# One Trainium2 core, attention block with mixture of experts: w_out kept whole and split early, token tiles of the output product finished one by one, diff-head work moved off VectorE, expert loads chained

## The chip, the cores and the metric

The program runs on one core of one Trainium2 chip. The metric is device time in microseconds (us) for one execution; the median of three runs is given. A profile of one execution comes with it: busy time of TensorE (PE, its weight loads PEld), VectorE (DVE), ScalarE (ACT), GpSimd (POOL), the queue of SyncE (SP) that issues most DMAs, and what the 16 DMA engines moved.

## The reference

One encoder layer, batch 1, 512 tokens, width 1024, all float32. Cut to what matters:

```python
h = rms_norm(x, attn_norm_w)
z = h @ w_in                       # 1024 x 5664: c_q, c_kv, k_rope, dq, dk, dv, g_mla, g_diff
o_mla  = latent_attention(...)     # 16 heads, width 64
# differential attention: 8 heads, two softmax maps of width 64 each, value width 128
a = softmax(q1 k1^T/8 - slope*|t-s|) - lam * softmax(q2 k2^T/8 - slope*|t-s|)
o_diff = rms_norm(a @ v, diff_subln_w) * (1 - lam_init)      # per head
merged = sigmoid(g_mla + b) * o_mla + sigmoid(g_diff + b) * o_diff
x = x + merged @ w_out             # 1024 x 1024
h2 = rms_norm(x, ffn_norm_w)
affinity = softmax(h2 @ router_w)  # 16 experts
gate, idx = top_k(affinity^T, 64)  # every expert picks its 64 tokens
for e in range(16):                # width 1024 -> 2048 -> 1024
    ye = (silu(h2[idx[e]] @ w_gate[e]) * (h2[idx[e]] @ w_up[e])) @ w_down[e] * gate[e]
    x[idx[e]] += ye
```

The expert weights are 16 x 3 x 8 MB, 402.7 MB in all, and each byte is read once.

## The kernel before

Products ahead of the routing are made in three matmuls each (`proj3`): both operands are split into a rounded part `hi` and a rest `lo`, and hi*hi, hi*lo and lo*hi are summed. A weight is split after it is loaded: ScalarE copies the hi part (L129, for diff weights L516), VectorE or GpSimd subtracts it for lo (L130, L517).

The program goes through these stages: projections and the 16 latent-attention heads with the gates (to about 315 us); differential attention, 8 heads (to 576 us); the product with `w_out` (`wo`, 518 to 609 us); routing and top-k (to 630 us); the experts (to the end).

**Differential heads.** A generator `proj` makes the projections `dqkv` of a head, one token tile of 128 tokens (24 matmuls) at a step, ahead of the attention of that head; it is 7 token tiles ahead when the first head starts. A head transposes its keys and queries (`kT` L550, `qT` L554), splits them (`KH`, `KL`, `QS`, the copy L560 on GpSimd), and for each of 4 token tiles t makes scores `S`, the biased maximum (L579), two exponentials (L581), the difference (L587, `pr`), the transposes `ATp`, copied out as `AT` (ScalarE for odd t, VectorE for even), and `pvd`. GpSimd makes the bias (L571) and the normed `qk` (L536). A head ends with `o` scaled by its norm (L610), transposed (`oT` L613), gated (L614) and added into `mrg` (L615), the merged output, transposed, one 128x512 tile for each head.

**w_out.** The weight is loaded in quarters of each half n of its columns, and split; `mt` is the hi and lo of `mrg` in pieces (L716 ScalarE, L717 VectorE). For n = 0 all token tiles are taken with the first seven k, then with the last, which is head 7's; for n = 1 the tiles t follow one another, 24 matmuls each, and each goes on to its residual sum (L745), transposes `xmT`, logits `lg` and affinities.

**Experts.** The weights come as 384 chunks of 1 MB, each in a slot of a ring. `ORDER` gives the 22 slots by letter: m, e, a, h, b, c, x are memory regions that become free at different times. All chunk loads (L702) go through SP's queue, in the order of use; a load waits until the last reader of its slot is done, and what stands behind it in the queue waits too. The four h slots hold `mt`, one token tile each. An expert takes 24 chunks: 16 for gate and up (`gu`), 8 for down (`y`).

Of the kernel before, what the change touches and what calls it, by code (L numbers as in the profile page):

```python
# [31 lines left out]
ORDER = "eeeemmaxaaaahhhhbbbbbc"  # L32
NRE, NRA, NRB = (ORDER.count(c) for c in "eab")
# [13 lines left out]
def build(tc, A, out):  # L47
# [41 lines left out]
    with ExitStack() as es:  # L89
# [9 lines left out]
        wpool = prj.enter_context(tc.tile_pool(name="w", bufs=1, reuse_waits="tile"))  # L99
# [406 lines left out]
        def diff_proj(h):  # L506
# [27 lines left out]
            eng = V if h == 0 else G  # L534
# [10 lines left out]
        def diff_head(h, qkv, qk2, gB):  # L545
# [22 lines left out]
            for t in range(NT):  # L568
# [36 lines left out]
        def finish(h, o, oss, gB):  # L605
# [20 lines left out]
        xm = xpool.tile([128, NT, D], F32, name="xm")  # L626
        for t in range(NT):
            SY.dma_start(xm[:, t], x_in[t * 128:(t + 1) * 128])
# [19 lines left out]
        pb.__exit__(None, None, None)  # L648
        pb3.close()

# [4 lines left out]
        wpool = att.enter_context(tc.tile_pool(name="wo", bufs=1, reuse_waits="tile"))  # L655

        def wo_view(n, i):
            return w_out[:, 2 * i:2 * i + 2, n * 512:(n + 1) * 512]

        def wo_split(n):  # L660
            return [w_split(wo_view(n, i), (128, 2, 512), eng=G if n == 0 and i == 3 else None,
                            raw=raw1[:, i - 2] if n == 1 and i > 1 else None) for i in range(4)]

        sc = wpool.tile([NE, 1024], F32, name="sc")
        wo0 = wo_split(0)
        mt_ = [ringH.tile([128, 2, KT, 128], F32R, name="mt", tag="wh", bufs=NT) for _ in range(NT)]
# [8 lines left out]
        rings = {"m": (lambda: mpool, "m8", 2), "e": (lambda: ringE, "we", NRE), "a": (lambda: ringA, "wa", NRA),  # L675
                 "b": (lambda: ringB, "wb", NRB), "h": (lambda: ringH, "wh", NT), "c": (lambda: ringC, "wc", 1),
                 "x": (lambda: ringX, "wx", 1)}
# [4 lines left out]
        def slot_tile(pool, tag, n, shape=(128, FF)):  # L682
            return pool().tile(list(shape), F32, name="w" + tag, tag=tag, bufs=n)

        def chunks():

            i = 0
            for e in range(NE):
# [3 lines left out]
                for src in srcs:  # L692
                    pool, tag, n = rings[order[i]]
                    i += 1
                    w = slot_tile(pool, tag, n)
                    if len(src.shape) == 3:
                        w = w.rearrange("p (j d) -> p j d", j=2)
                    if e == NE - 1 and src is srcs[-1]:
                        for j in range(2):
                            SY.dma_start(w[:, j], src[:, j])  # L700
                    else:
                        SY.dma_start(w, src)  # L702
                    yield w

        stream = chunks()
        early = [next(stream) for _ in range(5)]
        raw1 = slot_tile(*rings["a"], shape=(128, 2, 2, 512))
        for i in range(2):
            SY.dma_start(raw1[:, i], wo_view(1, 2 + i))
        early += [next(stream) for _ in range(2)]  # L710
# [75 lines left out]
        for n in range(2):  # L786
            wo = wo0 if n == 0 else wo_split(1)
            if n == 0:
                wps = [ps_tile(g_, "wo") for g_ in ("pj", "pj", "s", "s")]
                for ks in (range(7), range(7, 8)):  # L790
                    for t in range(NT):
                        wo_part(wps[t], t, wo, ks)
# [227 lines left out]
```

## Time and profile before

| | |
|---|---|
| median of 3 runs | 1559.41 us (1558.34 to 1559.48) |
| profiled execution, time | 1559.79 us |
| its span | 1558.1 us |
| PE / DVE / ACT / POOL busy | 1429.8 / 566.7 / 376.9 / 157.1 us |
| HBM read / written | 441.57 / 5.77 MB |

The span is what the trace holds between first and last instruction; the execution's own time is 1.7 us longer. In the rows below, busy time is a sum over instructions, a row's "idle before" is what its engine waited just ahead of it, and the name behind the arrow is what ended that wait. Matmul durations overlap, so the spacing of their starts is the rate.

### The profile page before, as it was taken

Reading aid. Unit: us, or ns where it says so; the run is one execution under the profiler, and the core shown is the slowest. Engines: PE = TensorE matmul, PEld = TensorE weight load, DVE = VectorE, ACT = ScalarE, POOL = GpSimd, SP = SyncE. Lnnn points to the kernel's source line nnn. Section 1 sums busy time; section 2 is a strip of 40 time slices with the busy share of each in tenths; the row PEclk is TensorE's granted clock in tenths of the full one; section 3 lists DMA queues with packets and bytes.
Section 4 is the critical chain, followed back from the end, with each engine's and each line's share of the span. In section 5 each row is a group of like instructions: output and inputs, shape, how many; then the busy total and the mean of one; then the engine's idle time right before and its main releaser. Section 6 shows DMA issues by size and latency. Waiting matters only on the chain. (4 is left out here: it accounts for less than half of the span.)

```text
span 1558.1 us, 18428 instructions
## 1 busy us (share of the span) xinstructions
PE 1429.8 (92%) x7119; PEld 778.1 (50%) x7119; DVE 566.7 (36%) x1412; ACT 376.9 (24%) x830; POOL 157.1 (10%) x213
## 2 busy tenths in 40 slices
PE   7999999999999897999999979889979979979876
PEld 6777767689888675434343333233224224215211
DVE  8965656448888887102102002002002002002100
ACT  4555545546565642000000000000000000000000
POOL 3003303023434410000000000000000000000000
PEclk9999999999999998999999999999999999999999
DMA  4412213132222268899999999999999999999997
GB/s 157 136 44 62 58 51 104 34 92 69 58 58 55 76 254 317 326 420 425 420 420 425 419 420 425 423 422 422 420 423 423 419 424 423 422 424 419 420 418 287
DMA packets 125690, 448.55 MB, mean 288 GB/s; under 512 B 9733, under 2 KB 51777, under 8 KB 92578
## 3 DMA queue, kind: packets, MB, share of 16 engines
q1 hardware_dynamic: 124160, 444.30, 71.7%
q0 software_dynamic: 1440, 3.07, 0.7%
q8 instruction: 56, 0.92, 0.2%
q14 instruction: 32, 0.26, 0.1%
q10 hardware_dynamic: 2, 0.00, 0.0%
HBM read 441.57 MB, written 5.77 MB: 287 GB/s over the span
## 5 line engine op out<-in xcount | busy, mean ns | idle before, releaser
L962 DVE TENSOR_TENSOR hh<-hh,gu 128x512 f32<-128x512 f32 x32 | 22.0, 687 | 433.3 <-PE gu L950 433.3
L950 PE MATMUL gu<-wwa,xeT 128*64 128x512 f32 x560 | 131.5, 605 | 13.6 <-DMA wwa<-in_expert_w_up_dram 7.0
L950 PE MATMUL gu<-wwb,xeT 128*64 128x512 f32 x520 | 121.6, 599 | 15.7 <-DMA wwb<-in_expert_w_up_dram 8.2
L950 PE MATMUL gu<-wwe,xeT 128*64 128x512 f32 x496 | 117.9, 603 | 15.5 <-DMA wwe<-in_expert_w_up_dram 8.9
L950 PE MATMUL gu<-wwh,xeT 128*64 128x512 f32 x432 | 101.3, 599 | 11.3 <-DMA wwh<-in_expert_w_gate_dram 6.5
L959 ACT ACTIVATE hh<-gu 128x512 f32<-128x512 f32 x32 | 19.0, 597 | 344.6 <-PE gu L950 344.6
L950 PEld LDWEIGHTS gu<-wwa,xeT 128*64 128x64 f32 x560 | 37.8, 137 | 103.0 <-issue 66.0
L201 PE MATMUL dqkv<-hl,hTh 128*128 128x384 f32 x256 | 88.5, 346 | 0.2 <-DVE hl L517 0.2
L200 PE MATMUL dqkv<-hl,hTh 128*128 128x384 f32 x256 | 87.3, 342 | 0.0
L889 POOL DMA_DIRECT2D out_dram<-acc x4 | 2.2, 558 | 830.0 <-DVE acc L885 830.0
L202 PE MATMUL dqkv<-hl,hTl 128*128 128x384 f32 x256 | 85.5, 338 | 0.0
L950 PEld LDWEIGHTS gu<-wwb,xeT 128*64 128x64 f32 x520 | 34.6, 136 | 100.5 <-issue 59.6
L983 PE MATMUL y<-wwb,hh 128*64 128x512 f32 x320 | 74.1, 599 | 7.2 <-DMA wwb<-in_expert_w_down_dram 7.2
L950 PEld LDWEIGHTS gu<-wwe,xeT 128*64 128x64 f32 x496 | 32.6, 137 | 94.6 <-issue 53.3
L970 ACT ACTIVATE hh<-hTp 128x512 f32<-128x512 f32 x16 | 9.6, 598 | 277.4 <-PE hTp L967 277.4
L950 PEld LDWEIGHTS gu<-wwh,xeT 128*64 128x64 f32 x432 | 28.7, 136 | 80.8 <-issue 51.1
L983 PE MATMUL y<-wwa,hh 128*64 128x512 f32 x280 | 63.7, 597 | 4.0 <-DMA wwa<-in_expert_w_down_dram 4.0
L911 PE MATMUL xeTp<-ohr,xm 128*128 128x128 f32 x512 | 62.6, 282 | 1.3 <-DVE ohr L898 1.3
L911 PEld LDWEIGHTS xeTp<-ohr,xm 128*128 128x128 f32 x512 | 59.8, 196 | 7.6 <-issue 6.3
L882 PE MATMUL comb<-yo 128*128 128x512 f32 x112 | 57.4, 625 | 4.1 <-ACT yo L995 4.1
L996 DVE COPY yo<-y 64x512 f32<-64x512 f32 x14 | 9.7, 694 | 140.3 <-ACT yo L995 140.3
L983 PE MATMUL y<-wwh,hh 128*64 128x512 f32 x240 | 55.1, 598 | 3.5 <-DMA wwh<-in_expert_w_down_dram 3.5
(356 smaller groups left out, 2548.4 us busy)
## 6 DMA issues: line engine op xcount, KB each, us to landing
wwb<-in_expert_w_down_dram SPq DMA_DIRECT2D x39, 1024.0 KB, 18.0
wwa<-in_expert_w_gate_dram SPq DMA_DIRECT2D x36, 1024.0 KB, 19.8
wwb<-in_expert_w_up_dram SPq DMA_DIRECT2D x35, 1024.0 KB, 19.5
wwa<-in_expert_w_down_dram SPq DMA_DIRECT2D x35, 1024.0 KB, 19.9
wwa<-in_expert_w_up_dram SPq DMA_DIRECT2D x34, 1024.0 KB, 19.8
wwe<-in_expert_w_gate_dram SPq DMA_DIRECT2D x32, 1024.0 KB, 19.6
wwb<-in_expert_w_gate_dram SPq DMA_DIRECT2D x30, 1024.0 KB, 19.6
wwe<-in_expert_w_up_dram SPq DMA_DIRECT2D x30, 1024.0 KB, 19.6
```

The costliest lines, as they stand in the source:

```text
L200: PE.matmul(p, sh, mh, start=first and k == 0, stop=False)
L201: PE.matmul(p, sh, ml, start=False, stop=False)
L202: PE.matmul(p, sl, mh, start=False, stop=last and k == n - 1)
L882: PE.matmul(p, ohT[:, t * 128:(t + 1) * 128], ysp[:, n], start=True, stop=True)
L889: G.dma_start(out2[t * 128:(t + 1) * 128], acc[t // 2][:, t % 2])
L911: PE.matmul(p[:, k], xm[:, t, kk * 128:(kk + 1) * 128], ohr[:, t].rearrange("p a s -> p (a s)"), start=t == 0, stop=t == NT - 1)
L950: PE.matmul(pp[j][hf * 64:(hf + 1) * 64], cur[:, k, par_ * 64:(par_ + 1) * 64], wt[:, hf * 1024 + j * 512:hf * 1024 + (j + 1) * 512], star ...
L959: S.activation(hid[:, j * 512:(j + 1) * 512], pp[j], AF.Silu)
L962: V.tensor_tensor(hs, hs, gu[1][j], OP.mult)
L970: S.activation(dst, p, AF.Copy)
L983: PE.matmul(y[a * 64:(a + 1) * 64], hT[:, f, hf * 64:(hf + 1) * 64], wt[:, j, a * 512:(a + 1) * 512], start=kt == 0, stop=kt == 15)
L996: V.tensor_copy(ysp[own, 1], y[64:])
```

## The change

`w_out` is loaded whole, in two transfers of 2 MB into the region that later holds `xm` (the reloaded x). It is kept as hi and lo in four pairs of k: pairs 0 and 1 are split right behind the latent attention (ScalarE, GpSimd) into a new region of four ring slots w; pairs 2 and 3 near the last two heads, into the b slots. `mt` is split a head at a time, whole 128x512 tiles; lo of heads 0 to 5 is on GpSimd. The reload of x moves behind the last reader of the raw `w_out`.

For token tiles 0 and 1 the product over k 0 to 5 is made early, halved by ScalarE and added to `xm` by GpSimd; for tile 2 it stays in PSUM. Behind head 7 tiles 0, 1, 2 take only k 6 and 7 and tile 3 takes all, and each tile goes to its logits before the next.

In each diff head the scaling of `o` moves from VectorE to ScalarE (four 128x128), the sum into `mrg` to GpSimd for heads 0 to 5, all `AT` copies of heads 6 and 7 to ScalarE, and `qk` of head 7 from GpSimd to VectorE. `proj` is one token tile less ahead. The pool of weights is closed behind the latent attention and a new one opened, so that diff weights wait for the last gate matmul. The ring has 23 slots, in another order, each load is bound to stand behind the one before it, and the scratch of GpSimd's DMAs is 4 KB.

```diff
-ORDER = "eeeemmaxaaaahhhhbbbbbc"
+ORDER = "mxeeaaaaambbbbwwwwhhhhc"
...
+        prjw.close()
+        wpool = prjw.enter_context(tc.tile_pool(name="w2", bufs=1, reuse_waits="tile"))
...
-            eng = V if h == 0 else G
+            eng = V if h in (0, 7) else G
...
-                if t % 2:
+                if t % 2 or h > 5:
                     S.activation(AT, p, AF.Copy)
...
-            V.tensor_tensor(o, o, ro[:, :, None].to_broadcast([128, NT, 128]), OP.mult)
             p = ps_tile("tr", "oT")
             for t in range(NT):
+                S.activation(o[:, t], o[:, t], AF.Copy, scale=ro[:, t:t + 1])
                 PE.transpose(p[:, t * 128:(t + 1) * 128], o[:, t], ident)
             V.scalar_tensor_tensor(gB, p, col(SUB), gB, OP.mult, OP.mult)
-            V.tensor_tensor(mrg(h), mrg(h), gB, OP.add)
+            (V if h > 5 else G).tensor_tensor(mrg(h), mrg(h), gB, OP.add)
...
-        for _ in range(2):
-            next(proj)
+        next(proj)
...
+        def wo_pair(i, pool, tag, raw):
+
+            hi, lo = (pool.tile([128, 2, D], F32R, name="wo", tag=tag, bufs=NR[tag[1]]) for _ in range(2))
+            for k in range(2):
+                S.activation(hi[:, k], raw[k], AF.Copy)
+                (G if k or i < 2 else V).tensor_tensor(lo[:, k], raw[k], hi[:, k].bitcast(F32), OP.subtract)
+            return hi, lo
...
+        SY.dma_start(raw, w_out[:, 0:4])
+        wo_ = [wo_pair(i, ringW, "ww", [raw[:, 2 * i + k] for k in range(2)]) for i in range(2)]
+        raw = xpool.tile([128, NT, D], F32, name="raw", tag="xm", bufs=1)
+        SY.dma_start(raw, w_out[:, 4:8])
...
+        def mt_split(c):
+            hi, lo = mth[c // 4][:, c % 4], mtl[c // 4][:, c % 4]
+            S.activation(hi, mrg(c), AF.Copy)
+            (G if c < 6 else V).tensor_tensor(lo, mrg(c), hi.bitcast(F32), OP.subtract)
...
+        for c in range(4):
+            mt_split(c)
+        wo_ += [wo_pair(i, ringB, "wb", [raw[:, 2 * i - 4 + k] for k in range(2)]) for i in range(2, 4)]
+        xm = xpool.tile([128, NT, D], F32, name="xm", tag="xm", bufs=1)
+        for t in range(NT):
+            xload = SY.dma_start(xm[:, t], x_in[t * 128:(t + 1) * 128])
+        for c in (4, 5):
+            mt_split(c)
+
+        for t in range(2):
+            for n in range(2):
+                p = ps_tile("pj", "wo")
+                wo_part(p, t, n, range(6))
+                part = mo2.tile([128, 512], F32, name="part", tag="ohr" if n else "oh", bufs=1)
+                S.activation(part, p, AF.Copy, scale=0.5)
+                xs = xm[:, t, n * 512:(n + 1) * 512]
+                G.tensor_tensor(xs, xs, part, OP.add)
+        wp2 = [ps_tile("pj", "wo") for n in range(2)]
+        for n in range(2):
+            wo_part(wp2[n], 2, n, range(6), last=False)
+        for c in (6, 7):
+            mt_split(c)
...
+            d = SY.dma_start(dst, src)
+            tc.add_manual_dep(d.ins, queued[0].name,
+                              mybir.DependencyInfo(mybir.DependencyClass.NoSync, mybir.DependencyReason.DATA),
+                              reason="in the order of use")
...
+        for t in range(NT):
+            wps = wp2 if t == 2 else [ps_tile("s", "wo") for n in range(2)]
+            xT = xTs[:, t % 2]
+            for n in range(2):
+                wo_part(wps[n], t, n, range(8) if t == 3 else range(6, 8), first=t != 2)
+                if n:
+                    xm_part(t, 0, 4, xT, S)
+                wo_evac(wps[n], t, n, 1 + n)
+            xm_part(t, 4, 2, xT, V)
+            xm_part(t, 6, 2, xT, S)
+            route(t, xT)
...
-    nc = bacc.Bacc("TRN2", target_bir_lowering=False, num_devices=1)
+    nc = bacc.Bacc("TRN2", target_bir_lowering=False, num_devices=1, dynamic_dma_scratch_size=4096)
```

The order of each engine's instructions moves at three places. First, SP's queue from the last pieces of `w_out` to the last slot that is filled for the first time; `ww` and a letter is a chunk in that slot, `wm` one in an m slot. Before:

```order
L127 DMA wr<-in_w_out_dram 128x2x512 x4
L702 DMA wm_6081<-in_expert_w_gate_dram 128x2048
L702 DMA wwx<-in_expert_w_gate_dram 128x2048
L702 DMA wwe<-in_expert_w_gate_dram 128x2048 x4
L709 DMA wwa<-in_w_out_dram 128x2x512 x2
L702 DMA wm_6086<-in_expert_w_gate_dram 128x2048
L702 DMA wwa<-in_expert_w_gate_dram 128x2048
L702 DMA wwa<-in_expert_w_up_dram 128x2048 x4
L702 DMA wwh<-in_expert_w_up_dram 128x2048 x4
L702 DMA wwb<-in_expert_w_down_dram 128x2x1024 x5
L702 DMA wwc<-in_expert_w_down_dram 128x2x1024
```

And of the change, from the reload of x on (`L730` is the load of a chunk there):

```order
L688 DMA xm<-in_x_dram 128x1024 x4
L730 DMA wm_6262<-in_expert_w_gate_dram 128x2048
L730 DMA wwx<-in_expert_w_gate_dram 128x2048
L730 DMA wwe<-in_expert_w_gate_dram 128x2048 x2
L730 DMA wwa<-in_expert_w_gate_dram 128x2048 x4
L730 DMA wwa<-in_expert_w_up_dram 128x2048
L730 DMA wm_6280<-in_expert_w_up_dram 128x2048
L730 DMA wwb<-in_expert_w_up_dram 128x2048 x4
L730 DMA www<-in_expert_w_up_dram 128x2048 x2
L730 DMA www<-in_expert_w_down_dram 128x2x1024 x2
L730 DMA wwh<-in_expert_w_down_dram 128x2x1024 x4
L730 DMA wwc<-in_expert_w_down_dram 128x2x1024
```

Ahead of the b slots stand ten chunks now, and all slots from b on (13) held `w_out`, `mt` or the transposed tiles `xT`; before, sixteen chunks stood ahead of the b slots, the last four in slots of `mt`.

Second, GpSimd around head 7, from the gate's product L541 (L545 in the change) on. Before:

```order
L541 TENSOR_SCALAR gB<-gB 128x512
L536 TENSOR_TENSOR qk_5730<-qkv,rq_y 128x256 x4
L130 TENSOR_TENSOR hl<-wr,hl 128x1024
L560 COPY KH<-KH 64x512
L571 TENSOR_SCALAR bias<-dist 128x512 x2
```

And of the change, where L676 is lo of `mt`, L640 lo of `w_out`, L699 the early sums into `xm`:

```order
L545 TENSOR_SCALAR gB<-gB 128x512
L676 TENSOR_TENSOR mt<-mrg,mt 128x512 x2
L575 TENSOR_SCALAR bias<-dist 128x512 x2
L676 TENSOR_TENSOR mt<-mrg,mt 128x512 x2
L640 TENSOR_TENSOR wo<-raw,wo 128x1024
L564 COPY KH<-KH 64x512
L640 TENSOR_TENSOR wo<-raw,wo 128x1024
L676 TENSOR_TENSOR mt<-mrg,mt 128x512 x2
L575 TENSOR_SCALAR bias<-dist 128x512 x2
L699 TENSOR_TENSOR xm<-xm,part 128x512 x4
```

The copy and the bias of head 7 stand behind splits that VectorE made before, and `qk` is gone from the queue.

Third, TensorE at the seam between latent and differential attention, at the last gate matmuls. Before:

```order
L444 MATMUL PTp<-ident,pr 128x128 x4
L201 MATMUL S<-kT,qT 128x512
L202 MATMUL S<-kT,qT 128x512
L202 MATMUL gate<-hTh,hl 128x512
L444 MATMUL PTp<-ident,pr 128x128 x4
L200 MATMUL dqkv<-hl,hTh 128x384
L201 MATMUL dqkv<-hl,hTh 128x384
```

And of the change:

```order
L203 MATMUL gate<-hTh,hl 128x512
L445 MATMUL PTp<-ident,pr 128x128 x4
L432 MATMUL qkT<-ident,kn 96x128 x4
L432 MATMUL qkT<-ident,q 96x128 x4
L201 MATMUL S<-kT,qT 128x512
L202 MATMUL S<-kT,qT 128x512
L203 MATMUL S<-kT,qT 128x512 x2
L201 MATMUL dqkv<-hl,hTh 128x384
```

The first `dqkv` stood directly behind the last gate matmul and one group of transposes; now eight more transposes and nine score matmuls stand between them.

## Rows read from the trace of the kernel before

**Rows 1.** Stretches: length, busy PE, PEld, DVE, ACT, POOL; PEclk; DMA share; GB/s

```profile
400.00:450.00 50.00, 48.60 (x295) 44.01 (x294) 45.23 (x126) 32.06 (x76) 20.59 (x17) 1.00 0.25 67
...
520.70:576.50 55.80, 47.29 (x237) 36.50 (x238) 49.48 (x134) 31.35 (x79) 18.02 (x13) 0.94 0.50 182
576.50:609.00 32.50, 32.50 (x183) 26.90 (x182) 22.10 (x84) 13.88 (x41) 0.00 (x0) 1.00 0.73 291
...
629.80:660.00 30.20, 30.20 (x153) 12.98 (x154) 4.02 (x10) 1.09 (x2) 0.00 (x0) 0.98 0.86 309
660.00:1540.00 880.00, 802.07 (x3682) 284.51 (x3680) 106.94 (x159) 39.92 (x67) 3.92 (x5) 1.00 1.02 422
```

**Rows 2.** SP's queue in order of time: start us, us, line, tile and source

```profile
550.84 0.34 SPq L702 DMA_DIRECT2D wm<-in_expert_w_gate_dram  x1
...
578.69 6.98 SPq L702 DMA_DIRECT2D wwa<-in_expert_w_up_dram  x4
588.05 21.34 SPq L702 DMA_DIRECT2D wwh<-in_expert_w_up_dram  x4
612.22 3.37 SPq L702 DMA_DIRECT2D wwb<-in_expert_w_down_dram  x5
615.62 0.53 SPq L702 DMA_DIRECT2D wwc<-in_expert_w_down_dram  x1
632.30 3.32 SPq L702 DMA_DIRECT2D wwe<-in_expert_w_down_dram  x2
```

**Rows 3.** DMAs issued from 609 to 632: KB each, us from issue to landing

```profile
wwc<-in_expert_w_down_dram SPq DMA_DIRECT2D x1, 1024.0 KB, 14.2
```

**Rows 4.** PE in order of time: last projection, last six matmuls of `wo`

```profile
520.20 0.34 PE L202 MATMUL dqkv<-hl,hTl 128*128 128x384 f32 x1
...
607.51 0.39 PE L200 MATMUL wo<-hl,mt 128*128 128x512 f32 x1
...
608.65 0.39 PE L202 MATMUL wo<-hl,mt 128*128 128x512 f32 x1
```

**Rows 5.** PE by line and shape, 520.4 to 576.5

```profile
L200 PE MATMUL wo<-hl,mt 128*128 128x512 f32 x31 | 12.8, 420 | 0.1
```

**Rows 6.** PE in head 7, in order of time: `kT`, last `ATp` and `pvd`, `oT`

```profile
538.41 0.38 PE L550 MATMUL kT<-ident,qk 128*128 128x128 f32 x2
...
566.98 0.60 PE L590 MATMUL ATp<-ident,pr 128*128 128x128 f32 x4
568.34 1.08 PE L598 MATMUL pvd<-qkv,AT 128*128 128x128 f32 x8
574.38 0.63 PE L613 MATMUL oT<-ident,o 128*128 128x128 f32 x4
```

**Rows 7.** VectorE by line and shape, 520.7 to 576.5

```profile
L130 DVE TENSOR_TENSOR hl<-wr,hl 128x1024 fp32r<-128x1024 f32 x5 | 6.6, 1327 | 0.0
...
L717 DVE TENSOR_TENSOR mt<-mrg,mt 128x256 fp32r<-128x256 f32 x12 | 5.5, 483 | 0.0
```

**Rows 8.** VectorE's step L608 in heads 6 and 7, GpSimd during the first

```profile
543.78 2.17 DVE L608 TENSOR_SCALAR vo<-oss 128x4 f32<-128x4 f32 x1 [0.30 <-ACT junk L601]
...
570.35 0.17 DVE L608 TENSOR_SCALAR vo<-oss 128x4 f32<-128x4 f32 x1 [0.53 <-ACT junk L601]
...
543.53 2.39 POOL L130 TENSOR_TENSOR hl<-wr,hl 128x1024 fp32r<-128x1024 f32 x1 [2.96 <-ACT hl L129]
```

**Rows 9.** PE at the seam, in order of time: last gate matmul, first `dqkv`

```profile
297.06 0.40 PE L202 MATMUL gate<-hTh,hl 128*128 128x512 f32 x1
...
297.67 0.42 PE L200 MATMUL dqkv<-hl,hTh 128*128 128x384 f32 x1
```

**Rows 10.** Diff weights, 250 to 320: split (ns min/median/max), and landing

```profile
L516 ACT ACTIVATE hl<-wr x4: 840/856/867, 251.0 to 297.6; 128x768 fp32r<-128x768 f32 x4
L517 DVE TENSOR_TENSOR hl<-wr,hl x4: 943/958/1167, 251.9 to 298.5; 128x768 fp32r<-128x768 f32 x4
...
DMA to landing us min/median/max: 2.5/2.6/4.8
```

More of the change, by code (lines that the diff above doesn't have):

```diff
@@ L29 @@
 NE, CAP, FF = 16, 64, 2048
-ORDER = "eeeemmaxaaaahhhhbbbbbc"
-NRE, NRA, NRB = (ORDER.count(c) for c in "eab")
+ORDER = "mxeeaaaaambbbbwwwwhhhhc"
+NR = {c: ORDER.count(c) for c in ORDER}
 NPR = NE // 2
@@ L647, in build @@
             pass
+        prjw.close()
+        prj.close()
+        ringH = es.enter_context(tc.tile_pool(name="ringH", bufs=1, reuse_waits="tile"))
+        mo2 = es.enter_context(tc.tile_pool(name="moe2", bufs=1, reuse_waits="tile"))
+        ringB = es.enter_context(tc.tile_pool(name="ringB", bufs=1, reuse_waits="tile"))
+        mth, mtl = ([ringH.tile([128, KT // 2, T], F32R, name="mt", tag="wh", bufs=NR["h"]) for _ in range(2)]
+                    for _ in range(2))
+        def mt_split(c):
+            hi, lo = mth[c // 4][:, c % 4], mtl[c // 4][:, c % 4]
+            S.activation(hi, mrg(c), AF.Copy)
+            (G if c < 6 else V).tensor_tensor(lo, mrg(c), hi.bitcast(F32), OP.subtract)
@@ new lines, in wo_part @@
+        def wo_part(p, t, n, ks, first=True, last=True):
+            q, d = slice(t * 128, (t + 1) * 128), slice(n * 512, (n + 1) * 512)
+            proj3(p, [(mth[k // 4][:, k % 4, q], mtl[k // 4][:, k % 4, q]) for k in ks],
+                  [(wo_[k // 2][0][:, k % 2, d], wo_[k // 2][1][:, k % 2, d]) for k in ks], first, last)
+        for c in range(4):
+            mt_split(c)
+        wo_ += [wo_pair(i, ringB, "wb", [raw[:, 2 * i - 4 + k] for k in range(2)]) for i in range(2, 4)]
+        xm = xpool.tile([128, NT, D], F32, name="xm", tag="xm", bufs=1)
@@ L660, in wo_split @@
[L660 to L666, printed above, removed]
+        ringC = es.enter_context(tc.tile_pool(name="ringC", bufs=1, reuse_waits="tile"))
+        sc1 = mo2.tile([NE, 512], F32, name="sc", tag="oh", bufs=1)
@@ L667, in build @@
+        sc2 = mo2.tile([NE, 320], F32, name="sc", tag="ohr", bufs=1)
         ringX = es.enter_context(tc.tile_pool(name="ringX", bufs=1, side="right", reuse_waits="tile"))
@@ L680, in build, with load @@
         order += lap * (3 * KT * NE // len(lap))
[L682 to L683 removed]
+        queued = [xload.ins]
+        def load(dst, src):
+            d = SY.dma_start(dst, src)
+            tc.add_manual_dep(d.ins, queued[0].name,
+                              mybir.DependencyInfo(mybir.DependencyClass.NoSync, mybir.DependencyReason.DATA),
+                              reason="in the order of use")
+            queued[0] = d.ins
         def chunks():
@@ L692, in chunks @@
                 for src in srcs:
-                    pool, tag, n = rings[order[i]]
+                    pool, tag = rings[order[i]]
+                    w = pool.tile([128, FF], F32, name="w" + tag, tag=tag, bufs=NR[order[i]])
                     i += 1
-                    w = slot_tile(pool, tag, n)
                     if len(src.shape) == 3:
@@ L699, in chunks @@
                         for j in range(2):
-                            SY.dma_start(w[:, j], src[:, j])
+                            load(w[:, j], src[:, j])
                     else:
-                        SY.dma_start(w, src)
+                        load(w, src)
                     yield w
+        xTs = ringC.tile([128, 2, KT, 128], F32, name="xT", tag="wc", bufs=NR["c"])
         stream = chunks()
[L706 to L710, printed above, removed]
-        stream = chain(early, stream)
-        for c0, c1 in ((0, 2), (2, 4), (4, 6), (6, 7), (7, 8)):
-            for t in range(NT):
-                hi, lo = mt_[t][:, 0, c0:c1], mt_[t][:, 1, c0:c1]
-                m = mrgs[c0 // 4][:, c0 % 4:(c1 - 1) % 4 + 1, t * 128:(t + 1) * 128]
-                S.activation(hi, m, AF.Copy)
-                V.tensor_sub(lo, m, hi.bitcast(F32))
+        early = [next(stream) for _ in range(10)]
+        stream = chain(early, stream)
         lt = cst.tile([128, 128], BF16, name="lt")
```

57 lines of the change are left out of this document (12 added, 45 removed).

## The prediction

> **What bounds the kernel now.** The first view is the table of stretches [rows 1]. From 660 to 1540 us the DMA engines are full (share 1.02, 422 GB/s) while TensorE (PE) is busy 802 of 880 us. A chunk of 1 MB (1.0486 million bytes) takes 1.0486/0.422 = 2.485 us, and there are 384. So the end is set by how early the stream of chunks runs without a pause. Ahead of 660 it does not: 291 GB/s from 576.5 to 609, 309 from 629.8 to 660. The second view, SP's queue, says why [rows 2]. Twelve chunks are issued from 550.84 to 578.69 (wm twice, wwx, wwe four, wwa five; only the first and the last are shown). The four wwh loads take from 588.05 to 609.4, because each slot still holds `mt` of a token tile that `wo` has to read. Six more follow by 615.62; the last lands 14.2 us later [rows 3], at 629.8. Only at 632.30 is a slot free again.
>
> That gives an account of the end. At 629.8, 22 chunks have landed and 362 are left: 362 x 2.485 = 899.6 us, while 1558.1 - 629.8 = 928.3 us were needed. Of the 28.7 us more, 30.2 x (1 - 309/422) = 8.1 us were lost up to 660 with a full ring [rows 1]. The other 20.6 us are other traffic, slower last loads and the work behind the last load; I carry them over unchanged.
>
> The third view is PE in order of time: the last projection `dqkv` ends at 520.5, the last `wo` matmul at 608.9 [rows 4]. Between them lies what PE waits for. From 576.5 to 609 it is busy all the time at a granted clock of 1.00; from 520.7 to 576.5 it is busy 47.3 of 55.8 us at a mean clock of 0.94, that is, partly at 1.2 instead of 2.4 GHz, and VectorE 49.5 [rows 1], so VectorE is the fuller of the two.
>
> **What PE loses there.** Starts of `wo` are 0.228 us apart (607.51 to 608.65 is five steps [rows 4]); the record of one is 0.39, so a record is longer than its place by 0.16. 91 `wo` matmuls (31 of the first kind [rows 5], 30 of each other) make 20.7 us; five token tiles of scores `S`, six matmuls of the same size each, 6.8; eight groups of ATp (0.60 - 0.16) and pvd (1.08 - 0.16) [rows 6] 10.9; three groups of oT at 0.47 1.4; kT and qT at the same price 0.9. Together 40.7 us of 56.0, so 15.3 us are lost, to waits, to the lower clock they bring, and to the run-in of matmuls behind gaps.
>
> **The change part by part.**
>
> *The order of loads.* Ten chunks stand ahead of the first b slot. They wait for steps of heads 6 and 7; the last, the second m slot, for the split of `mt` of head 7. The thirteen slots from b on are free only when token tile 3, the last one, has passed `wo`. Let R be the end of that last `wo` (608.9 before). Ten chunks have landed by then, as nothing holds them longer than head 7, and 374 follow without a pause: thirteen more fill the ring at R + 32.3, but the first expert starts at about R + 20.9 (629.8 - 608.9) and frees a slot 2.5 later (632.30), so the ring is not full when the stream needs it. End of span = R + 374 x 2.485 + 20.6 = R + 950.0. The present 1558.1 is met at R = 608.1. So the account hangs on R alone, one us for one us, and the longer hold on the last slots is already in it: five chunks fewer than before have landed at R (15 then), which costs 12.4 us and is paid by the 8.1 us of full ring and by the pause before 612.22.
>
> *The number of matmuls* is the same: 192 `wo` before and after. R moves by what PE loses, and by nothing else.
>
> *Head 7.* kT to oT takes 36.0 us now [rows 6]. In that time VectorE also makes splits of `mt` (5.5 us, all in this stretch) and two or more splits of w_out (1.33 each, 2.5 taken [rows 7]), and one step that takes 0.17 us elsewhere takes 2.17 [rows 8]. All this goes elsewhere: 36.0 - 5.5 - 2.5 - 2.0 = 26.0. The scaling of o moves to ScalarE at no gain on the path, as it stays a step before oT. Added is GpSimd: the copy KH of head 7 stands behind four mt splits, two bias tiles and one w_out split. The trace has a split of 128x1024 at 2.39 [rows 8], so one of 128x512 is estimated at 1.2. The mt splits can't start before the last projection, whose memory they take. Four of them and one of w_out are 7.2 us plus bias; I add 2 us, with ends of 0 and 7. So 28 us.
>
> *From the last dqkv to kT of head 7*: 18.2 us now (520.2 to 538.4). The step needs the norm and four qk products, and VectorE has less of everything else; bounds 6 and 12, I take 8, nearer to the low end because qk no longer waits on GpSimd. oT of head 7 is then 36 us behind the last dqkv. PE's own work up to there is 69 `wo`, 24 `S`, six groups of ATp and pvd, oT, kT and qT: 15.7 + 5.5 + 8.2 + 1.8 = 31.2. Loss 4.8 us. Behind head 7 each of tiles 0 to 2 has only twelve `wo` matmuls to cover its residual sum and transposes, where there were 24; I add 1.2 us. Loss after: 6 us, ends 2 and 11.
>
> *The projections run less far ahead.* Heads start a token tile (24 matmuls) earlier, and the last dqkv comes later by the attention work moved ahead of it; the two cancel in R.
>
> *The seam.* The first dqkv stands 0.6 us behind the last gate matmul now [rows 9], with its weights loaded long before. In the change the first load waits for that matmul: 2.6 to land, 0.86 and 0.96 to split [rows 10], 4.4 us, against some 3 us of transposes and scores that PE has left (nine scores at 0.228, two groups at 0.47). Two staging buffers hold pairs 3 and 4 a further 4.4 us, in which 12 dqkv of the first pairs and the rest of the latent heads run. I take 3 us, with ends 0 and 7.
>
> *Per-head VectorE work* falls by two 0.68 us passes in six heads (only the scaling in the last two). PE is busy 48.6 of 50 us there [rows 1], so little can come of it: 1.5 us, ends 0 and 4. The early splits of pairs 0 and 1 lie beside projections, and the smaller DMA scratch touches transfers of GpSimd off the path; I cost both at nothing. Without cover the early splits would be four times 2.39 us of GpSimd ahead of the first bias.
>
> *Sum.* R = 608.9 - 15.3 + 6 + 3 - 1.5 = 601.1. Span 1551.1; with the 1.7 us around it 1552.8, against 1559.8 of the profiled execution. The median shown is 0.4 us lower, so **1552.4 us**. With each term at its ends together R would be 590 to 612; two in three terms near the middle give 1549 to 1557.
>
> **The rivals.**
>
> *PE never waits (1544).* The seam is hidden by the latent heads' end, and PE loses 1 us: R = 608.9 - 15.3 + 1 - 1.5 = 593.1, time 1544.4. For it: 108 `wo` matmuls are free of head 7. Against: 39 of them stand behind the last oT in PE's order, so they can't fill a gap in front of it.
>
> *The gain is given back (1559).* The seam costs its 7 us, and head 7's kT comes at 12 instead of 8: R = 601.1 + 4 + 4 = 609, time 1560. For it: all weights of the first diff head were there early before, now none is. The bounds are 1556.3 and 1562.5, 0.2% around the median, about what a measurement of this kernel tells from no change.
>
> *GpSimd stops VectorE: slower (1564).* While GpSimd ran one split of 2.39 us, a VectorE step of 0.17 us took 2.17 [rows 8]. The change puts six mt splits (7.2 us by the estimate) and two w_out splits (4.8) on GpSimd behind the last dqkv. If VectorE stands still for all 12.0, R = 613.1, time 1564.4; the four sums into xm (4.8) would follow at the tiles' end. It decides from 7.0 us of standstill (608.1 - 601.1). Against: VectorE worked through most of the 18.0 us of GpSimd in that stretch [rows 1]. The Trainium skill (SBUF — State Buffer, "Who interferes with whom") says that the two share a pair of ports as an exclusive lock, held for the whole instruction, and that issue order decides which blocks. By that rule, each new GpSimd subtraction that meets a VectorE operation of the named kinds holds it until its end, as the row of 2.17 us shows once; no row here shows how often.
>
> **How the numbers follow.** Likeliest (1549 to 1557): 0.54. PE never waits: 0.17. Given back: 0.15. Slower: 0.14. Faster by over 0.2% (below 1556.3) is the first but 0.05, and the second: 0.66. Within 0.2%: 0.05 and 0.14 of the third, 0.19. Slower: 0.15. The range is 1544 to 1562: it leaves out about half of the second and most of the last, 0.2 in all.
>
> **What would show it.** Right: the last `wo` near 601; the b loads of SP's queue issue there and no gap follows; 422 GB/s from then on without a dip up to 660; kT to oT of head 7 near 28 us. Wrong: a wait of the first dqkv on its weights above 7 us; the KH copy or bias on GpSimd as what PE or VectorE waits for in head 7; VectorE steps of 0.2 us that last 1 to 2 us beside GpSimd; a full ring behind R, which would mean that PE and not the loads starts the stream.

## The result and the profile after

The changed kernel takes 1573.76 us (median of 4 runs, 1573.15 to 1575.62) against 1558.88 of the kernel before on the same chip: the ratio is 1.0094, 95% interval 1.0082 to 1.0107. It is slower by about 15 us: outside the range of 1544 to 1562, and not faster, as was forecast. The span of the profiled execution is 1571.4 us.

The stretches of the changed kernel, as in [rows 1], cut at its own marks (last `dqkv`, last `oT`, last `wo`, first expert); the columns are length, busy time with instructions of PE, PEld, DVE, ACT and POOL, granted clock, DMA share and GB/s:

```profile
330.00:335.00 5.00, 1.32 (x8) 1.00 (x7) 1.28 (x8) 0.84 (x1) 0.00 (x0) 1.00 0.95 332
335.00:342.00 7.00, 6.80 (x30) 6.48 (x30) 3.44 (x8) 1.61 (x3) 0.00 (x0) 0.76 0.44 112
534.80:582.30 47.50, 35.77 (x176) 27.05 (x174) 39.77 (x97) 29.10 (x71) 24.55 (x17) 0.93 0.43 159
582.30:621.60 39.30, 38.97 (x206) 31.71 (x207) 22.78 (x86) 12.13 (x40) 1.30 (x1) 1.00 0.34 136
621.60:642.90 21.30, 8.41 (x52) 7.23 (x50) 15.53 (x73) 3.62 (x9) 0.00 (x0) 0.61 1.00 412
642.90:660.00 17.10, 17.10 (x90) 8.04 (x90) 1.75 (x6) 0.00 (x0) 0.00 (x0) 0.98 1.03 425
660.00:1540.00 880.00, 803.11 (x3692) 284.82 (x3691) 107.40 (x160) 40.51 (x68) 3.92 (x5) 1.00 1.02 422
```

The stream of chunks behaves as described: no dip from 642.9 on, where [rows 1] has 309 GB/s. But it restarts later. SP's queue, as in [rows 2]: the tenth chunk is issued at 587.01, and the first b load has to wait until 620.20.

```profile
587.01 0.33 SPq L730 DMA_DIRECT2D wm<-in_expert_w_up_dram  x1
620.20 2.24 SPq L730 DMA_DIRECT2D wwb<-in_expert_w_up_dram  x4
622.54 0.94 SPq L730 DMA_DIRECT2D www<-in_expert_w_up_dram  x2
```

PE in order of time, the marks that answer to [rows 4] and [rows 6]: first `kT` of head 0, of head 6, last `dqkv`, `kT` and `oT` of head 7, last `wo`.

```profile
342.15 0.27 PE L554 MATMUL kT<-ident,qk 128*128 128x128 f32 x1
...
518.78 0.27 PE L554 MATMUL kT<-ident,qk 128*128 128x128 f32 x1
...
534.58 0.42 PE L203 MATMUL dqkv<-hl,hTl 128*128 128x384 f32 x1
...
548.40 0.45 PE L554 MATMUL kT<-ident,qk 128*128 128x128 f32 x1 [3.83 <-DVE qk L540]
...
582.31 0.33 PE L617 MATMUL oT<-ident,o 128*128 128x128 f32 x1 [1.36 <-ACT o L616]
...
621.37 0.39 PE L203 MATMUL wo<-wo,mt 128*128 128x512 f32 x1
```

So R, the end of the last `wo`, is 621.6 (621.37 + 0.23) instead of 601.1, and R + 950.0 would be 1571.6: the account of the end holds, and the whole miss lies ahead of R. Three places show. First, head 0's `kT` comes at 342.2, 1.6 us later than before although one token tile (24 matmuls) less stands ahead of it; PE is busy 1.3 of 5 us from 330 on, and at a clock of 0.76 behind it. Second, from the first `kT` of head 0 to that of head 6 ("heads 0 to 6" below) it is 176.6 us where it was 173.8 (340.59 to 514.36). Third, from the last `dqkv` to `oT` of head 7 it is 47.7 us, where the prediction had 36.

What VectorE and GpSimd do ahead of `kT` of head 7 and ahead of its scores, in order of time:

```profile
543.22 1.26 DVE L67 TENSOR_TENSOR rq_a<-rq_a,rq_y 128x16 f32<-128x16 f32 x1
544.51 1.19 DVE L68 SCALAR_TENSOR_TENSOR rq_y<-rq_a,rq_y 128x16 f32<-128x16 f32 x1
545.74 3.19 DVE L540 TENSOR_TENSOR qk<-qkv,rq_y 128x256 f32<-128x256 f32 x3
...
558.44 1.22 DVE L62 TENSOR_SCALAR ro_y<-vo 128x4 int32<-128x4 int32 x1
559.70 1.19 DVE L66 SCALAR_TENSOR_TENSOR ro_a<-vo,ro_y 128x4 f32<-128x4 f32 x1
560.92 0.16 DVE L67 TENSOR_TENSOR ro_a<-ro_a,ro_y 128x4 f32<-128x4 f32 x1
```

```profile
542.79 2.89 POOL L676 TENSOR_TENSOR mt<-mrg,mt 128x512 fp32r<-128x512 f32 x2
545.63 2.35 POOL L640 TENSOR_TENSOR wo<-raw,wo 128x1024 fp32r<-128x1024 f32 x1
...
558.34 2.53 POOL L676 TENSOR_TENSOR mt<-mrg,mt 128x512 fp32r<-128x512 f32 x2
```

Four small steps last 1.2 us each while GpSimd subtracts; the next, at 560.92 when GpSimd is done, lasts 0.16. The three `qk` products at 545.74 take 3.19 us instead of 3 x 0.41. It is the row of 2.17 us of [rows 8] again, now several times over, and PE waits 3.83 us for `qk` (the row at 548.40). The prediction had named such steps as a sign of being wrong.

### The profile page after: what moved, and what is told of

It is laid out like the page before. It is cut to its first block, busy times and chain, and to the rows that moved or that the text cites. A ratio compares the mean times of both kernels' runs of the same rounds, so it can differ in the third digit from the quotient of the medians.

```text
span 1571.4 us, 18398 instructions
## 1 busy us (share of the span) xinstructions
PE 1433.8 (91%) x7119; PEld 778.4 (50%) x7119; DVE 562.8 (36%) x1382; ACT 386.7 (25%) x858; POOL 181.8 (12%) x223
## 4 chain that ended last, share of the span: by engine, by line
PE 51%; DMA 30%; DVE 10%; issue 5%; ACT 3%; POOL 0%; SPq 0%; POOLq 0%; DVEq 0%; ACTq 0%
PE gu L975 13%; PE y L1008 6%; DMA wwb<-in_expert_w_gate_dram 4%; DMA wwh<-in_expert_w_up_dram 4%; PE xeTp L936 3%; DMA wwa<-in_expert_w_up_dram 3%; DMA wwa<-in_expert_w_gate_dram 3%; DMA www<-in_expert_w_up_dram 3%; DMA wwh<-in_expert_w_gate_dram 3%; PE comb L907 2%; DMA wwe<-in_expert_w_down_dram 2%; DMA wwb<-in_expert_w_down_dram 2%; DMA www<-in_expert_w_down_dram 2%; DMA wwh<-in_expert_w_down_dram 2%; PE PTp L445 2%
## 5 line engine op out<-in xcount | busy, mean ns | idle before, releaser
L975 PE MATMUL gu<-wwa,xeT 128*64 128x512 f32 x544 | 127.6, 600 | 17.5 <-DMA wwa<-in_expert_w_up_dram 9.2
L975 PE MATMUL gu<-www,xeT 128*64 128x512 f32 x424 | 99.0, 599 | 13.2 <-DMA www<-in_expert_w_up_dram 7.1
L975 PE MATMUL gu<-wwb,xeT 128*64 128x512 f32 x432 | 101.0, 599 | 8.0 <-DMA wwb<-in_expert_w_up_dram 4.6
L984 ACT ACTIVATE hh<-gu 128x512 f32<-128x512 f32 x32 | 19.1, 597 | 342.2 <-PE gu L975 342.2
L975 PE MATMUL gu<-wwh,xeT 128*64 128x512 f32 x392 | 91.4, 600 | 10.4 <-DMA wwh<-in_expert_w_gate_dram 6.8
L975 PEld LDWEIGHTS gu<-www,xeT 128*64 128x64 f32 x424 | 28.3, 136 | 82.5 <-issue 46.6
L975 PEld LDWEIGHTS gu<-wwb,xeT 128*64 128x64 f32 x432 | 29.0, 136 | 76.8 <-issue 53.0
L1008 PE MATMUL y<-wwa,hh 128*64 128x512 f32 x256 | 58.9, 597 | 2.2 <-DMA wwa<-in_expert_w_down_dram 2.1
L975 PE MATMUL gu<-wwe,xeT 128*64 128x512 f32 x224 | 53.7, 599 | 5.6 <-DMA wwe<-in_expert_w_up_dram 3.9
```

The lines of the kernel that those rows point to most:

```text
L975: PE.matmul(pp[j][hf * 64:(hf + 1) * 64], cur[:, k, par_ * 64:(par_ + 1) * 64], wt[:, hf * 1024 + j * 512:hf * 1024 + (j + 1) * 512], star ...
L984: S.activation(hid[:, j * 512:(j + 1) * 512], pp[j], AF.Silu)
L1008: PE.matmul(y[a * 64:(a + 1) * 64], hT[:, f, hf * 64:(hf + 1) * 64], wt[:, j, a * 512:(a + 1) * 512], start=kt == 0, stop=kt == 15)
```

## The experiments

Times below are medians; where an interval matters it stands beside them. R and other marks are from each run's profile. The first stages differ between executions: of two kernels that are alike up to there, one had its first `kT` at 340.6 and one at 343.3. So a difference of R below 3 us says little by itself, and a profiled execution can lie almost 3 us from its run's median. The length of heads 0 to 6 is steadier: it is 173.6 to 173.8 us in the three runs with the heads of before, and 176.4 to 176.8 in the five with all of the changed ones.

**Is it GpSimd's late splits?**

```diff
-            (G if c < 6 else V).tensor_tensor(lo, mrg(c), hi.bitcast(F32), OP.subtract)
+            V.tensor_tensor(lo, mrg(c), hi.bitcast(F32), OP.subtract)
-                (G if k or i < 2 else V).tensor_tensor(lo[:, k], raw[k], hi[:, k].bitcast(F32), OP.subtract)
+                (G if i < 2 else V).tensor_tensor(lo[:, k], raw[k], hi[:, k].bitcast(F32), OP.subtract)
```

> The changed kernel with all late splits back on VectorE: lo of mt for heads 0 to 5 and lo of the w_out pairs 2 and 3, which GpSimd made. In the changed kernel the last wo matmul ends at 621.6 us and the time is 1573.8. Theory A, GpSimd's two-input subtractions stop VectorE: its steps from 530 us on last 11.6 us longer than the same steps elsewhere, most of that ahead of kT and QS of head 7. Without them that excess falls under 3 us; VectorE itself gets 6 x 0.68 + 2 x 1.22 = 6.5 us more, part of it on the path. Last wo at 612 to 617, time 1564 to 1569. Theory B, VectorE is simply full and every us put on it counts: last wo at 625 to 628, time 1577 to 1580. Theory C, the finishing tile by tile and the seam made it slower: time within 3 us of 1573.8.

Measured: 1569.16 us, R 617.7. Theory A in direction, just above its bounds; B is refuted, since 6.5 us more on VectorE made the kernel 4.6 us faster; C, less than 3 us, falls too. VectorE in that run, where the same steps stand beside its own splits:

```profile
546.41 0.16 DVE L67 TENSOR_TENSOR rq_a<-rq_a,rq_y 128x16 f32<-128x16 f32 x1
546.49 1.21 DVE L640 TENSOR_TENSOR wo<-raw,wo 128x1024 fp32r<-128x1024 f32 x1
547.63 0.16 DVE L68 SCALAR_TENSOR_TENSOR rq_y<-rq_a,rq_y 128x16 f32<-128x16 f32 x1
```

Held against the median of their kind from 345 us on, VectorE's steps behind 530 us are 0.8 us longer in all here, and 11.4 in the changed kernel: the standstill is gone. kT to oT of head 7 is 27.6 us there (548.70 to 576.29), where it was 33.9; but kT still comes 12.7 us behind the last `dqkv` (13.8 in the changed kernel).

> As the run with the late splits on VectorE, and also qk of head 7 back on GpSimd, as in the kernel before. Theory A: GpSimd is idle then, so four products of 0.6 to 1.0 us on it replace four of 0.41 on VectorE; kT of head 7 comes 0 to 2 us later or, if VectorE is the fuller engine, up to 2 us earlier; time within 2 us of the run with the splits alone. Theory B: 1.6 us less on VectorE, time 1.6 us shorter.

The edit is `eng = V if h == 0 else G` on top of the first one. Measured: 1569.82 us, within 2 us of the run above, as theory A has it. With the splits on VectorE no difference shows between the two engines for `qk` of head 7.

**The sum into mrg, in the changed kernel.** `V.tensor_tensor(mrg(h), mrg(h), gB, OP.add)` for all heads.

> The changed kernel with the sum into mrg of heads 0 to 5 back on VectorE. The first kT of heads 0 and 6 are 176.6 us apart in the changed kernel and 173.8 before. Theory A: the sum on GpSimd (1.9 us, ahead of the bias in its queue) holds VectorE or the bias, and the period comes back: 1.5 to 3 us off the time, 1571 to 1572. Theory B: PE sets the period, VectorE's 0.68 us a head are hidden either way: no change, within 1 us of 1573.8.

Measured: 1573.38 us; heads 0 to 6 take 176.7 us. Theory B: the sum is hidden there.

**The seam: the reopened pool alone, on the kernel before.**

```diff
+        prjw.close()
+        wpool = prjw.enter_context(tc.tile_pool(name="w2", bufs=1, reuse_waits="tile"))
```

> The kernel before with one part of the change alone: the pool of weights is closed behind the latent attention and a new one opened, so that diff weights are loaded only behind the last gate matmul. Theory A, the seam costs what the changed kernel shows (its first kT comes 1.6 us later than before though it waits for 24 matmuls, 4.2 us, less: 5.8 us): first kT at 345 to 347, last wo 4 to 6 us later, time 1563 to 1565.5. Theory B, the latent heads' end covers it when 168 projections stand ahead: within 1.5 us of 1558.9.

Measured: 1558.18 us, ratio 0.9992 (0.9982 to 1.0002); first `kT` at 341.31, 0.7 us later. Theory B: the wait of the first weights on the last gate matmul is covered. So the loss at the seam of the changed kernel is something else. SP's queue there, the landing of the weights of 326 to 329 us, and PE:

```profile
325.10 0.38 SPq L648 DMA_DIRECT2D raw<-in_w_out_dram  x1
326.77 1.03 SPq L515 DMA_DIRECT2D wr<-in_w_in_dram  x2
...
SPq L648 <- POOL wo L640: 8.4, 1, 8.4
...
DMA to landing us min/median/max: 6.5/6.5/6.6
```

```profile
334.79 0.44 PE L201 MATMUL dqkv<-hl,hTh 128*128 128x384 f32 x1 [3.68 <-ACT hl L520]
```

The second half of `w_out` goes where the first was. It waits 8.4 us at the head of SP's queue for GpSimd's fourth early split, which ends at 325.1; the last weights of head 1 are issued 1.7 us behind it, share the DMA engines with its 2 MB, and land only after 6.5 us.

**The second raw half behind the weights.** Its load is bound behind the weights of heads 1 and 2 and the first pair of head 3.

```diff
+                if h == 3:
+                    tc.add_manual_dep(raw_load.ins, w_load.ins.name,
+                                      mybir.DependencyInfo(mybir.DependencyClass.NoSync, mybir.DependencyReason.DATA),
+                                      reason="behind the diff weights")
```

> The changed kernel with the second raw half of w_out issued on SP behind the weights of diff heads 1 and 2 (and the first pair of head 3) instead of ahead of the last pair of head 1. In the changed kernel it waits on SP for GpSimd's fourth early split until 325.1 us, the weights of head 1 stand behind it, and PE waits 3.7 us for them at 334.8, at a lower clock after it. Theory A, this wait is the extra cost of the seam: first kT of head 0 at 337 to 339 instead of 342.15, last wo 4 to 5.5 us earlier (616 to 617.6), time 1568 to 1570. Theory B, the loss at the seam is the reopened pool: first kT stays at 342 and the time within 1.5 us of 1573.8.

Measured: 1569.91 us. First `kT` at 337.31, 4.8 us earlier, and the last `dqkv` 5.1 us earlier: theory A for the seam. The same weights in this run:

```profile
327.00 8.80 SPq L515 DMA_DIRECT2D wr<-in_w_in_dram  x8
...
DMA to landing us min/median/max: 2.5/2.7/3.4
```

They are issued no earlier (327.00 instead of 326.77), so the place in the queue had not held them; they land after 2.7 us instead of 6.5, and PE has no such wait. In the five runs with this order and six tiles ahead the first `kT` is at 337.2 to 338.0, in the four without it at 342.2 to 344.2, and in the kernel before with six tiles (below) at 337.7: nothing of the seam's loss is left. R came only 2.2 us earlier (619.4), short of the expectation; head 7 gave part of it back.

> Both repairs together: the second raw half behind the weights, and the late splits on VectorE. Theory A, the two losses lie in different stages and add up: 4.6 us from the splits and 4 to 5.5 from the weights, last wo at 612 to 614, time 1563.5 to 1565.5, still slower than the kernel before because the stretch from the last dqkv to the last wo (81.7 us with the splits on VectorE) doesn't shrink further. Theory B, they share the same slack: time no lower than 1568.

Both edits together. Measured: 1563.29 us, R 611.6: theory A, a little below its bounds. The two repairs take 10.5 of the 15 us. The ratio to before is 1.0025 (1.0015 to 1.0034), so something is left.

**The head moves, on the kernel before.** All four (o on ScalarE, sum on GpSimd, `AT` of heads 6 and 7, `qk` of head 7), then two of them alone.

> The kernel before with the per-head part of the change alone: o scaled on ScalarE, the sum into mrg on GpSimd for heads 0 to 5, AT of heads 6 and 7 on ScalarE, qk of head 7 on VectorE. Theory A, less VectorE work helps where VectorE is full (520 to 576 us, 49.5 of 55.8): last wo 2 to 5 us earlier, time 1554 to 1557. Theory B, these moves lengthen a head (29.0 to 29.5 us) by waits between engines: kT of heads 0 and 6 176 to 177 us apart instead of 173.8, last wo 1 to 4 us later, time 1560 to 1563.

> The kernel before with one head move alone: o scaled by ScalarE in four 128x128 steps. The run with all head moves had kT of heads 0 and 6 180.8 us apart instead of 173.8 and was 7.5 us slower. Theory A, the sum on GpSimd is the cause, as it is queued ahead of the next biases: here 174 or less, time within 1.5 us of 1559. Theory B, the four scalings hold ScalarE's exponentials and oT: 177 to 181, time 1562 to 1567.

> The kernel before with the other head move alone: the sum into mrg of heads 0 to 5 on GpSimd. Theory A, it is the cause of the longer heads: kT of heads 0 and 6 178 to 181 us apart, time 1564 to 1567. Theory B, it is hidden: 174, time within 1.5 us of 1559.

Measured: all moves 1566.97 us, heads 0 to 6 in 180.8 us: theory B, and more than it allowed. o on ScalarE alone: 1559.72 us (ratio 0.9996), 174.1 us. The sum on GpSimd alone: 1558.94 us (0.9990), 175.9 us: the heads are 2 us longer, the time is the same. Neither gives the 7 us by itself. `AT` of heads 6 and 7 and `qk` of head 7 come behind `kT` of head 6, so what lengthens heads 0 to 6 must be the other two moves together; no run has just these two, and `AT` and `qk` weren't tried alone.

**One more slot, on the kernel before.**

```diff
-ORDER = "eeeemmaxaaaahhhhbbbbbc"
+ORDER = "eeeemmaxaaaahhhhbbbbbbc"
```

and the 4 KB scratch.

> The kernel before with one more slot (a sixth b) and the 4 KB scratch. The account of the end says that before the change 8.1 us are lost to a full ring between 629.8 and 660. A 23rd chunk can land in that time: the time falls by up to one chunk, 2.5 us, to 1556 to 1557.5, with the last wo where it was (608.9). Rival: the smaller scratch holds GpSimd's DMAs, or the extra load holds nothing up and gains nothing: within 0.7 us of 1558.9 or above.

Measured: 1557.05 us against 1559.47, ratio 0.9981 (0.9971 to 0.9991): 2.4 us, as expected, about one chunk. The slot and the scratch weren't tried apart. In the profile R is 2.7 us later (611.6), not where it was, as the first `kT` already is (343.3); behind R the span is 4 us shorter, 945.2 us. On the kernel before this part of the change is a gain, and with it alone that kernel is faster than both.

**Repaired kernel, heads as before.** o and the sum on VectorE in all heads, on top of the two repairs.

> The changed kernel with the two repairs (raw behind the weights, late splits on VectorE) and, in all heads, o scaled and the sum into mrg made on VectorE again, as before. Theory A, these head moves lengthen a head: kT of heads 0 and 6 were 176.7 us apart with both repairs and 173.8 before; the distance returns to 173.5 to 174.5 and the time falls from 1563.3 to 1560 to 1561. Theory B, the longer head comes from the projections that run one token tile less ahead, or from PE: distance 176 to 177, time within 1 us of 1563.3.

Measured: heads 0 to 6 in 176.8 us, as theory B has it; time 1566.18 us, 3 us above the run with the repairs, which neither theory has. Theory A falls. The last two heads have 0.68 us more on VectorE each, in a stretch in which it is full; R is 1.8 us later. That this makes the 3 us isn't shown.

> As the run before it, with the lo parts of w_out pairs 2 and 3 (4 x 1.21 us on VectorE) bound to stand behind QS of head 7 in VectorE's queue; nothing else moves. With both repairs PE waited 2.7 and 0.6 us for QS, and its clock fell to 0.5 to 0.8 in the ten us behind it. Theory A, work that nobody needs yet stands ahead of head 7's chain: last wo 3 to 6 us earlier than without this edit, time 1555 to 1558. Theory B, the wait moves to the early products, which then lack their lo parts: time within 1.5 us of the run without it.

Measured: 1568.41 us, R 617.0. Neither theory: it is 2 us slower. kT of head 7 comes 10.3 us behind the last `dqkv` instead of 12.7, but PE still waits 2.9 us for QS (3.9 without this edit), and `oT` of head 7 comes 5 us later; the four splits now stand inside its softmax (560.9 to 566.1).

**Is VectorE's work the bound of the last stretch?** ScalarE writes zeros for the lo parts of pairs 2 and 3, so that the low part of half of `w_out` is left out of the product.

> The changed kernel with the two repairs, but the lo parts of w_out pairs 2 and 3 aren't computed: ScalarE writes zeros in their place (4 x 1.04 us), which leaves the low part of half of w_out out of the product. VectorE has 4 x 1.21 = 4.9 us less between the last dqkv and head 7's scores; number and order of matmuls stay. Theory A, VectorE's total work is the bound of that stretch: QS of head 7 comes 3 to 5 us earlier, the waits of PE for QS (3.9 us) go, the clock doesn't fall behind them, last wo at 605 to 608, time 1557 to 1560. Theory B, PE's order is the bound, or ScalarE becomes it: last wo at 610 to 613, time within 1.5 us of 1563.3.

Measured: 1565.39 us, R 613.7. VectorE and ScalarE there:

```profile
530.00:540.00 10.00, 8.62 (x46) 6.40 (x45) 8.78 (x31) 8.86 (x20) 4.84 (x3) 1.00 0.08 28
540.00:545.00 5.00, 4.32 (x29) 3.39 (x27) 3.18 (x14) 4.95 (x10) 0.00 (x0) 1.00 0.00 0
545.00:550.00 5.00, 0.81 (x3) 0.41 (x3) 4.39 (x11) 4.89 (x12) 0.60 (x1) 0.90 0.00 0
```

kT of head 7 comes 10.4 us behind the last `dqkv`, so VectorE's splits had taken 2.3 us there. From 540 to 545 VectorE has room (3.18 of 5 us), but ScalarE is now full (4.95 and 4.89 of 5), and PE waits 4.9 us for QS, where it waited 3.9: theory B in its second form, a little outside its bounds. The run doesn't say what VectorE alone would give; it says that there is no slack on ScalarE either.

**Why the heads are longer.** Seven tiles ahead in the repaired kernel; six ahead alone on the kernel before; seven ahead with the head moves undone in the repaired kernel. Six ahead is this edit of the kernel before:

```diff
-        for _ in range(2):
-            next(proj)
+        next(proj)
```

> The changed kernel with the two repairs (raw behind the weights, late splits on VectorE; 1563.3 us), and the projections seven token tiles ahead again instead of six. First kT of head 0 comes 4 us later (341.5). Theory A, running one tile less ahead is what makes the heads longer: kT of heads 0 and 6 are 173.5 to 174.5 us apart instead of 176.7, the last dqkv comes at 527 to 531 with less attention work ahead of it, and the time falls by 1 to 3 us, 1560 to 1562.5. Theory B, PE is full in the heads and the tile ahead only shifts work: distance 176 to 177, time within 1 us of 1563.3 or above.

> The kernel before with one part alone: projections six token tiles ahead instead of seven. Theory A, this makes the heads longer by itself: first kT 4 us earlier, kT of heads 0 and 6 176.5 to 177 us apart instead of 173.8, last wo 2 to 4 us later, time 1561 to 1563.5. Theory B, the heads are longer for another reason that only the changed kernel has (its early splits, its pools): distance 173.8, last wo unchanged, time within 1.5 us of the kernel before.

> The changed kernel with the two repairs, the head moves undone (o and the sum on VectorE) and seven tiles ahead. Theory A, with seven tiles ahead the heads have their old length when both moves are undone: distance 173.5 to 174.5, last dqkv at 526 to 528, time 1562 to 1565 against 1566.2 with six tiles. Theory B: distance 176 or more, so that something else in the changed kernel lengthens them; time 1566 or above.

Measured, heads 0 to 6: repaired kernel with seven tiles and the moves 181.6 us (1568.9 us; neither theory: longer, not shorter); before with six tiles 177.6 us (1562.05 us, ratio 1.0016, 1.0006 to 1.0026: theory A); repaired with seven tiles and moves undone 174.1 us (1566.16 us: theory A for the distance, not for the time). Put beside the runs above, in each pair first the kernel before, or the changed kernel for six tiles with the moves, then a repaired one:

```
tiles ahead   heads as before   o on ScalarE, sum on GpSimd
seven         173.8, 174.1      180.8, 181.6
six           177.6, 176.8      176.6, 176.7
```

The length of a head hangs on both parts. With the heads as before, six tiles ahead costs 2.7 to 3.8 us over heads 0 to 6; with the moves, seven is the worse. That is shown; which wait inside a head does it isn't: PE is busy 28 of 29 us both in the kernel before and in the repaired one, and none of its named waits reaches 2 us in three heads.

## Why the prediction was wrong, point by point

**The account of the end was right.** In the changed kernel and the ten variants of it with that order of slots (all runs above that start from the changed kernel), the span minus R is 949.6 to 950.0 us, against 950.0 predicted; it is 949.2 in the kernel before. R decides, one us for one us, and the ring isn't full behind it.

**Where the 20.5 us of R were missed.** Between the last `dqkv` and `oT` of head 7, 11.7 us: 47.7 instead of 36. Behind `oT` none: the sum has the 34.5 us of before, 22 more `wo` at 0.228 and the 1.2, in all 40.7, and it was 39.3. That leaves about 10 us ahead of the last `dqkv`: 2.8 at the first `kT` (342.2 instead of 340.6 - 4.2 + 3, with 4.2 us for 24 projections), 4.3 over heads 0 to 6 (176.6 instead of 173.8 - 1.5), the rest from there to the last `dqkv`. The sum with every term at its better end gives 591.6 and not 590, which changes nothing.

**The step that failed first: 2 us for GpSimd in head 7, as delay of its queue.** "If VectorE stands still" was only a rival, and it happened. What the runs showed is VectorE's own standstill: with GpSimd's splits gone kT to oT went from 33.9 to 27.6 us, and the time fell by 4.6 us alone and by 6.6 on top of the other repair (R by 3.9 and 7.8). That 27.6 lies beside the 28 predicted is in part luck: without GpSimd the sum had 26, with none of the 6.5 us that VectorE does there instead. The rival's 12 us of standstill was near the 11.4 us by which VectorE's steps were longer, but R lost less than that, against VectorE doing the work; its chance of 0.14 was too low. The rule of the Trainium skill (SBUF — State Buffer, "Who interferes with whom") agrees with these rows: the steps at 544.51 and 559.70 end at 545.70 and 560.89, GpSimd's pairs of splits at 545.68 and 560.87.

**The step costed at nothing: the early splits.** The text put them beside the projections and named only the bias as exposed. The load of the second half waits for them on SP, is issued just ahead of the last weights of head 1, and slows them on the DMA engines: 3.7 us of PE at 334.8 and a lower clock after it, 4.8 us at the first `kT`. The 3 us that the seam was given had been laid on the reopened pool, whose 0.7 us at the first `kT` lie within the spread of executions, and which costs nothing in the time. So the size was near and the mechanism wrong, and the loss was 3.9 to 5.9 us of the time (2.2 to 6.1 of R; with GpSimd's and with VectorE's splits).

**"The two cancel in R": the tile less ahead.** It doesn't cancel. Six tiles ahead alone make heads 0 to 6 take 177.6 us instead of 173.8, and the kernel before 1.9 us slower in the median.

**Per-head VectorE work, 1.5 us gained**: nothing. Neither of the two moves changes the time of the kernel before by more than can be measured, and all four head moves together cost it 7.5 us.

**From the last dqkv to kT of head 7, 8 us with bounds 6 and 12**: 13.8, and 12.7 without GpSimd's splits. This term was mis-sized, and its reason was wrong too. The 18.2 us of before go with seven tiles ahead: the kernel before with six has 11.8, the repaired kernel with seven 18.2 and, with the head moves undone, 18.1. So the fall from 18.2 is the last `dqkv` coming later, which the prediction had cancelled elsewhere, and not a lighter VectorE or `qk`. What the changed kernel has above the 8 is in part splits: those of `mt` and of `w_out` pairs 2 and 3 are made behind the last `dqkv`, and in the two runs without the latter's lo parts on VectorE ahead of QS the term is 10.3 and 10.4, inside its bounds. In the run with both repairs VectorE is busy nearly all the time ahead of the scores, ScalarE up to 540, and PE waits:

```profile
530.00:540.00 10.00, 8.62 (x44) 6.35 (x43) 9.62 (x31) 9.54 (x21) 4.89 (x3) 1.00 0.04 13
540.00:545.00 5.00, 4.54 (x27) 3.23 (x26) 4.92 (x14) 4.09 (x10) 0.00 (x0) 1.00 0.00 0
545.00:550.00 5.00, 1.58 (x4) 1.08 (x5) 4.58 (x8) 2.60 (x5) 0.60 (x1) 0.80 0.63 204
550.00:555.00 5.00, 5.00 (x13) 3.82 (x13) 4.34 (x20) 3.30 (x9) 2.98 (x2) 0.52 1.02 422
```

```profile
547.29 0.50 PE L584 MATMUL S<-KH,QS 128*128 128x512 f32 x1 [2.75 <-DVE QS L573]
```

**Behind head 7** PE is busy 38.97 of 39.3 us: the tiles that are finished one by one cover their own sums and transposes, within the 1.2 us that the sum gave them.

Left open: with both repairs the time is still 0.25% above that of the kernel before, and R 2.7 us later. The kernel before with six tiles alone comes close to it: its last `dqkv` is at 529.7 us (529.8 with both repairs), and from there to R it takes 81.1 us (81.8). So no gain of the early `w_out` products over that kernel shows behind the last `dqkv`. The tile less ahead and the full VectorE and ScalarE are shown to cost; that they add up to just this isn't, because putting the heads or the tile back moved the loss to the last stretch (from 81.8 to 89.8 us between the last `dqkv` and R in the run with seven tiles, some of it attention work that then lies behind the last `dqkv`).

## What to carry to other kernels

Work moved from a full VectorE to an idle GpSimd isn't off the path as long as VectorE makes small steps of a chain beside it: look in the profile for steps that last until GpSimd's instruction ends, and count those. A large load that waits for an engine is issued when that engine lets it, here just ahead of weights that were needed sooner, and it takes the DMA engines from them; for each load that a change adds, ask what is issued behind it and when. And take a change of many parts apart: here one more slot with the smaller scratch gained 2.4 us, while the whole change cost 15.

## What was not expected of the hardware

VectorE's steps on 16 or 4 elements a partition, 0.16 us alone, took 1.19 to 1.26 us each beside GpSimd's subtractions, one after another: a chain of such steps moves at the pace of GpSimd's instructions. It isn't so beside all of GpSimd's work: beside its bias, which reads one tensor (541.33 to 542.82 in the changed kernel), five of six small steps took 0.16 to 0.21 us and one 0.63. And the clock: in the rows of the repaired kernel above PE was busy 1.58 of 5 us, the granted clock was 0.80 in that stretch and 0.52 in the next, where PE was busy all the time; matmuls that start 0.23 us apart at full clock did so at about 0.43 us there (1.2 GHz). By an estimate from these rows, 5.00 x (1 - 0.52) = 2.4 us, the lower clock cost about as much again as the wait of 2.75 us ahead of it.
